# Seven-product pairs whose products add up in PSUM, and a sixth pair in the last projection

## The chip, the cores and the metric

The kernel runs on one core of one Trainium2 chip. The metric is the time of one execution on the device, in microseconds (us). TensorE (PE) does the matrix products into PSUM banks, VectorE (DVE) and ScalarE (ACT) read PSUM and do the elementwise work, GpSimd (POOL) and SyncE (SP) mainly issue transfers.

## The reference

Two layers over 640 tokens (512 latent, 128 context) with a model width of 2048. Each layer is a norm with a modulation, one wide input projection, two attention or convolution mixers with gates, an output projection, and a gated residual. What matters here is the output projection of each layer and its gated residual:

```python
    return jnp.concatenate([y_a, y_b], axis=-1) @ w_out, new      # even layer; the odd one alike
...
        xp = xp + gt_p * out_p
        xs = xs + gt_s * out_s
```

So both layers multiply a 640 x 2048 matrix y by a 2048 x 2048 matrix and add the product, times a gate for each column and token group, to x. The gate is one third of `modulation(...)`, a projection of the condition.

## The kernel before, in words

Everything is held transposed: features on the 128 partitions, the 640 tokens (`NT`) along the free dimension, in two halves of 320 (`HALF`). Accuracy near fp32 is had by splitting each operand into a high and a low part (`split`, L230 on ScalarE for the high part, L231 on VectorE for the low part) and using three matmuls: high x high, high x low, low x high. An output tile is 128 columns of the weights. A single tile (`proj_q`, L265 to L267) takes 16 slices of the contraction x 2 halves x 3 matmuls of 320 columns.

`project_out` (one call for each layer) runs the output projection. The first three tiles are led together while y comes in (`run_tiles`); then single tiles up to `N_SINGLE`, which is 4 in layer 0 and 6 in layer 1; then the other tiles in pairs (`run_pairs`): six pairs in layer 0, five in layer 1. A pair is two columns of tiles times two halves of tokens times two halves of the contraction, a 2 x 2 x 2 block product, done with seven products instead of eight by a Strassen-Winograd scheme. The seven are named Q1, Q2, N5, P6, P7, P4, Q3, and each is 8 slices x 3 matmuls (L515 to L517) into a bank of its own, in the order of the dictionary `MOV`. The weights enter as A11, A12, A21, A22 and as sums of them (`operand`, L451 to L461); the moving side are the halves of y (B11, B21, B22), the difference T1 and three sums T2, T3, T4.

`forms` makes T2 to T4 in eight steps: two loads of y from the scratch in HBM, four operations on VectorE (L1055 to L1058) and a split into the buffers T0 to T7. It runs as a generator in the queue `attn`, advanced between groups of matmuls of the leading tiles. In layer 1 it is put into the queue one group later (`y1_maker` at k = 4) than in layer 0 (`y0_maker` at k = 8 of the order 0, 2, 1, 3). T1 is split over one half of y (`t1`) when the last single tile has passed that half; for this the last single runs one half of the tokens and then the other. The room for `t1` and for what is kept between products are slices of `tables` (`room`).

What is done with a product stands in `after`: Q1 is copied to SBUF (L481), the others are combined on VectorE (L484 to L503) and added to the residual tile `xr` with the gate `hgt` (`res_sum`, L1072). Weight loads (`load8`, L427, in four buffers `w8`; `load_raw`, L243) are on SP, up to a pair ahead; splits are 3 half products ahead (`SPLIT_AHEAD`). When a pair of tiles is whole, layer 0 stores it and sums its squares (`x1_done`, `x1_last`), and layer 1 transposes and stores it (`rows_out`, `rows_last`). At the end of layer 0 the norm of the next layer follows half by half (`norm_half`), x1 is loaded back (`x1_tail`, `h1_maker`) and the next input projection begins.

The names are those of Tile's pools: instructions are put in order for each engine, and buffers handed out, when the program is built, so an engine's order follows the program with small shifts.

Of the kernel before, what the change touches and what calls it, by code (L numbers as in the profile page):

```python
# [20 lines left out]
P = 128  # L21
# [32 lines left out]
def trunk_kernel(ctx: ExitStack, tc: tile.TileContext, I: dict, O: dict):  # L54
# [81 lines left out]
    hgt = [const.tile([P, KT, 2], F32, name=f"hgt{l}") for l in range(2)]  # L136


    def ada_done(l, cb, h=0, n=4):
# [7 lines left out]
        elif which == 2:  # L147
            V.tensor_scalar(hgt[l][:, ks, :], mod[l][:, fs, :], 0.5, None, ALU.mult)

# [270 lines left out]
    def run_pairs(cols, w_ap, mov, room, begin, part, done, tail):  # L420
# [58 lines left out]
        def after(p, name, ps):  # L479
            if name == "Q1":  # L480
                A.copy(q1, ps)  # L481
                begin(p)
            elif name == "Q2":
                V.tensor_add(z, ps, q1)  # L484
                done(p, 0, 0, z)
            elif name == "N5":
                st8["n5"] = ps
            elif name == "P6":
                V.tensor_sub(u2, ps, q1)
                V.tensor_sub(u4, st8["n5"], u2)  # L490
                if p == len(cols) - 1:
                    part(p, 0, 1, u4)
            elif name == "P7":
                V.tensor_sub(z, ps, u4)
                done(p, 1, 1, z)
                V.tensor_add(u2, ps, u2)
                part(p, 1, 0, u2)
            elif name == "P4":
                done(p, 1, 0, ps)
            elif p == len(cols) - 1:  # L500
                done(p, 0, 1, ps)
            else:
                V.tensor_add(u4, ps, u4)  # L503
                done(p, 0, 1, u4)
# [4 lines left out]
        for i, (p, name) in enumerate(seq):  # L509
            ps, rows_ = pproj.tile([P, 512], F32, tag=f"p{'ab'[i % 2]}{i // 2 % 2}", name="pq")[:, 0:HALF], mov[MOV[name]]  # L510
            for h in range(2):
                wh, wl = parts[2 * i + h]
                for j in range(4):
                    hi, lo = rows_(4 * h + j)
                    PE.matmul(ps, wh[:, j, :], hi, start=(h == 0 and j == 0), stop=False)  # L515
                    PE.matmul(ps, wh[:, j, :], lo, start=False, stop=False)  # L516
                    PE.matmul(ps, wl[:, j, :], hi, start=False, stop=(h == 1 and j == 3))  # L517
# [971 lines left out]
```

## Time and profile before

| | us |
|---|---|
| median of three runs | 2333.07 (2333.01 to 2333.62) |
| the profiled execution | 2331.45 |
| its span in the profile | 2329.7 |
| TensorE busy | 2287.0 |
| VectorE busy | 1595.3 |
| ScalarE busy | 934.5 |
| GpSimd busy | 134.6 |
| pairs of layer 0, first matmul to last | 976.7 to 1126.1 |
| pairs of layer 1, first matmul to last | 2195.2 to 2324.8 |

The span runs from the first to the last instruction; the execution's own time has what lies around it too. Rows of the timeline begin with the start and the duration in us. A bracket at the end of a row tells how long the engine stood before it, and on what. In a view of groups, a row has the count, the busy time, the mean in ns, and the idle time ahead with the releaser. In a view of waits, a row has the sum, the count and the longest. The duration of a matmul's row reaches from its start to its modelled end, and rows of neighbouring matmuls overlap.

### The profile page before, as it was taken

Reading aid. Unit: us, or ns where it says so; the run is one execution under the profiler, and the core shown is the slowest. Engines: PE = TensorE matmul, PEld = TensorE weight load, DVE = VectorE, ACT = ScalarE, POOL = GpSimd, SP = SyncE. Lnnn points to the kernel's source line nnn. Section 1 sums busy time; section 2 is a strip of 40 time slices with the busy share of each in tenths; the row PEclk is TensorE's granted clock in tenths of the full one; section 3 lists DMA queues with packets and bytes.
Section 4 is the critical chain, followed back from the end, with each engine's and each line's share of the span. In section 5 each row is a group of like instructions: output and inputs, shape, how many; then the busy total and the mean of one; then the engine's idle time right before and its main releaser. Section 6 shows DMA issues by size and latency. Waiting matters only on the chain.

```text
span 2329.7 us, 41919 instructions
## 1 busy us (share of the span) xinstructions
PE 2287.0 (98%) x16116; PEld 2213.1 (95%) x16116; DVE 1595.3 (68%) x3270; ACT 934.5 (40%) x1963; POOL 134.6 (6%) x183
## 2 busy tenths in 40 slices
PE   7999999999999999999999999999999999999999
PEld 5889999999999999999999899999999999999999
DVE  4668887777777774988855755755856754568576
ACT  5334542433422222544554344444334444444343
POOL 1001000000000000000010100101000001000101
PEclk9999999999999999999999999999999999999999
DMA  9986345435455553844431422413423312128542
GB/s 322 293 263 200 102 116 176 146 105 171 128 169 166 170 165 124 274 135 137 152 98 55 132 82 70 145 52 98 120 72 97 103 46 82 46 74 274 179 121 70
DMA packets 399257, 321.99 MB, mean 138 GB/s; under 512 B 18882, under 2 KB 353184, under 8 KB 398544
## 3 DMA queue, kind: packets, MB, share of 16 engines
q1 hardware_dynamic: 391056, 288.94, 41.5%
q0 software_dynamic: 7280, 28.20, 3.3%
q8 instruction: 127, 2.08, 0.4%
q10 hardware_dynamic: 720, 2.16, 0.3%
q14 instruction: 74, 0.61, 0.1%
HBM read 290.79 MB, written 28.44 MB: 137 GB/s over the span
## 4 chain that ended last, share of the span: by engine, by line
PE 87%; DVE 5%; DMA 4%; ACT 2%; issue 1%; POOL 1%; SPq 0%; POOLq 0%; DVEq 0%; ACTq 0%
PE pa L265 10%; PE pb L266 10%; PE pb L265 10%; PE pb L267 10%; PE pa L266 10%; PE pa L267 10%; PE pq L515 4%; PE pq L517 4%; PE pq L516 4%; PE T L693 2%; PE S L705 2%; PE S L707 1%; PE S L706 1%; DMA yin<-yd 1%; PE T L167 1%
## 5 line engine op out<-in xcount | busy, mean ns | idle before, releaser
L230 ACT ACTIVATE wh<-raw 128x512 fp32r<-128x512 f32 (+1 forms) x510 | 307.4, 604 | 795.3 <-PE pb L266 673.5
L265 PE MATMUL pa<-h,wh 128*128 128x320 f32 x1760 | 561.9, 319 | 3.2 <-ACT h L230 1.6
L266 PE MATMUL pa<-h,wh 128*128 128x320 f32 x1760 | 547.2, 311 | 1.7 <-DVE h L231 1.6
L267 PE MATMUL pa<-h,wl 128*128 128x320 f32 x1760 | 545.8, 310 | 0.0
L267 PE MATMUL pb<-h,wl 128*128 128x320 f32 x1760 | 545.2, 310 | 0.0
L266 PE MATMUL pb<-h,wh 128*128 128x320 f32 x1760 | 544.9, 310 | 0.0
L265 PE MATMUL pb<-h,wh 128*128 128x320 f32 x1760 | 544.7, 310 | 0.0
L231 DVE TENSOR_TENSOR wl<-raw,wh 128x512 fp32r<-128x512 f32 (+1 forms) x510 | 333.3, 654 | 304.6 <-ACT wh L230 282.0
L202 DVE SCALAR_TENSOR_TENSOR acc<-adaw,sT,acc 128x512 f32<-128x512 f32 (+1 forms) x600 | 356.5, 637 | 23.3 <-DMA adaw<-in_ada_w 22.0
L265 PEld LDWEIGHTS pa<-h,wh 128*128 128x128 f32 x1760 | 331.9, 189 | 23.8 <-issue 17.0
L266 PEld LDWEIGHTS pa<-h,wh 128*128 128x128 f32 x1760 | 332.3, 189 | 4.9 <-DVE h L231 2.7
L267 PEld LDWEIGHTS pa<-h,wl 128*128 128x128 f32 x1760 | 331.9, 189 | 1.2 <-issue 1.2
L267 PEld LDWEIGHTS pb<-h,wl 128*128 128x128 f32 x1760 | 330.7, 188 | 0.8 <-issue 0.8
L266 PEld LDWEIGHTS pb<-h,wh 128*128 128x128 f32 x1760 | 330.6, 188 | 0.9 <-issue 0.8
L265 PEld LDWEIGHTS pb<-h,wh 128*128 128x128 f32 x1760 | 330.5, 188 | 0.7 <-issue 0.4
L679 ACT ACTIVATE p<-S,nm,rq 128x768 f32<-128x768 f32 (+3 forms) x120 | 101.2, 843 | 107.5 <-DVE nm L674 81.2
L515 PE MATMUL pq<-h,wh 128*128 128x320 f32 x352 | 109.9, 312 | 1.2 <-ACT wh L230 1.2
L516 PE MATMUL pq<-h,wh 128*128 128x320 f32 x352 | 108.8, 309 | 0.0
L517 PE MATMUL pq<-h,wl 128*128 128x320 f32 x352 | 108.5, 309 | 0.0
L672 DVE TENSOR_REDUCE nm<-S 128x1 f32<-128x768 f32 (+3 forms) x120 | 91.9, 765 | 21.7 <-PE S L707 20.2
L230 ACT ACTIVATE pth<-T 128x512 fp32r<-128x512 f32 (+1 forms) x132 | 66.0, 533 | 71.8 <-PE T L693 69.4
L231 DVE TENSOR_TENSOR ptl<-T,pth 128x512 fp32r<-128x512 f32 (+1 forms) x132 | 77.7, 608 | 6.7 <-ACT pth L230 5.4
(306 smaller groups left out, 3418.5 us busy)
## 6 DMA issues: line engine op xcount, KB each, us to landing
raw<-in_od_w_in SPq DMA_DIRECT2D x208, 256.0 KB, 2.9
adaw<-in_ada_w SPq DMA_DIRECT2D x192, 256.0 KB, 3.0
raw<-in_ev_w_in SPq DMA_DIRECT2D x176, 256.0 KB, 3.0
ada<-in_ada_w SPq DMA_DIRECT2D x32, 1024.0 KB, 7.7
adaw<-in_ada_w SPq DMA_DIRECT2D x128, 128.0 KB, 2.4
yd<-y POOLq DMA_DIRECT2D x34, 320.0 KB, 3.0
yin<-yd SPq DMA_DIRECT2D x32, 320.0 KB, 4.2
w<-yd SPq DMA_DIRECT2D x32, 320.0 KB, 4.1
```

The source lines that it names most:

```text
L202: V.scalar_tensor_tensor(out=a, in0=w, scalar=sT[:, kt, c:c + 1], in1=a, op0=ALU.mult, op1=ALU.add)
L230: A.activation(hi, x, AF.Copy)
L231: V.tensor_sub(lo, x, hi)
L265: PE.matmul(ps, wh[:, i, :], hi[:, sl], start=(j == js[0] if alone else (pos == 0 and j == 0)), stop=False)
L266: PE.matmul(ps, wh[:, i, :], lo[:, sl], start=False, stop=False)
L267: PE.matmul(ps, wl[:, i, :], hi[:, sl], start=False, stop=(j == js[1] - 1 if alone else (pos == 3 and j == 3)))
L515: PE.matmul(ps, wh[:, j, :], hi, start=(h == 0 and j == 0), stop=False)
L516: PE.matmul(ps, wh[:, j, :], lo, start=False, stop=False)
L517: PE.matmul(ps, wl[:, j, :], hi, start=False, stop=(h == 1 and j == 3))
L672: V.tensor_reduce(nm, s, axis=AX.X, op=ALU.max, negate=True)
L679: A.activation(p[:, 0:n], s, AF.Exp, scale=rsc, bias=nm, accum_out=l)
L693: PE.transpose(t[:, i * P:(i + 1) * P], p, ident)
```

## The change

The seven products get another order: Q1, N5, P6, Q2, P7, Q3, P4. Q1, P6, P7 and P4 add up in one bank (`pa0` or `pa1`, in turn from pair to pair), N5 and Q3 in `pb0`, Q2 in `pb1`. Only Q1, N5 and Q2 start a bank anew. Between the products of a chain ScalarE copies the partial sum to SBUF (after Q1, N5, P6 and P7), and VectorE adds copies where two chains meet (after Q2, P7 and Q3). For this the signs change: the forms T2 to T4 are made with other signs (two of the four operations are now `scalar_tensor_tensor`), the second tile of a pair comes out negated and takes a negated gate `nhgt`, and the two halves of the tokens swap roles (`HX`). The last product of a pair is P4 in place of Q3. The last single tile runs its halves in the other order. In layer 1 `N_SINGLE` becomes 4: two single tiles become a sixth pair. At the end of layer 0 the row of norm factors lies in `sf` in place of `T3`, and the reloads of x1 change buffers accordingly.

```diff
+            V.tensor_scalar(nhgt[l][:, ks, :], mod[l][:, fs, :], -0.5, None, ALU.mult)
...
-        MOV = {"Q1": "B11", "Q2": "B21", "N5": "T1", "P6": "T2", "P7": "T3", "P4": "T4", "Q3": "B22"}
+        MOV = {"Q1": "B11", "N5": "T1", "P6": "T2", "Q2": "B21", "P7": "T3", "Q3": "B22", "P4": "T4"}
+        BANK = {"N5": "pb0", "Q3": "pb0", "Q2": "pb1"}
...
-        q1, z, u2, u4 = room
+        q1, n5, u2, u3 = room
...
+            elif name == "N5":
+                A.copy(n5, ps)
+            elif name == "P6":
+                A.copy(u2, ps)
             elif name == "Q2":
-                V.tensor_add(z, ps, q1)
-                done(p, 0, 0, z)
-            elif name == "N5":
-                st8["n5"] = ps
-            elif name == "P6":
-                V.tensor_sub(u2, ps, q1)
-                V.tensor_sub(u4, st8["n5"], u2)
-                if p == len(cols) - 1:
-                    part(p, 0, 1, u4)
+                V.tensor_add(q1, ps, q1)
+                done(p, 0, 0, q1)
             elif name == "P7":
-                V.tensor_sub(z, ps, u4)
-                done(p, 1, 1, z)
+                A.copy(u3, ps)
+                V.tensor_add(n5, u3, n5)
+                done(p, 1, 1, n5)
+            elif name == "Q3":
                 V.tensor_add(u2, ps, u2)
-                part(p, 1, 0, u2)
-            elif name == "P4":
+                done(p, 0, 1, u2)
+            else:
                 done(p, 1, 0, ps)
-            elif p == len(cols) - 1:
-                done(p, 0, 1, ps)
-            else:
-                V.tensor_add(u4, ps, u4)
-                done(p, 0, 1, u4)
...
-            ps, rows_ = pproj.tile([P, 512], F32, tag=f"p{'ab'[i % 2]}{i // 2 % 2}", name="pq")[:, 0:HALF], mov[MOV[name]]
+            bank, rows_, new = BANK.get(name, f"pa{(p + 1) % 2}"), mov[MOV[name]], name in ("Q1", "N5", "Q2")
+            if new:
+                banks[bank] = pproj.tile([P, 512], F32, tag=bank, name="pq")[:, 0:HALF]
+            ps, kw = banks[bank], {} if new else {"skip_group_check": True}
...
-            elif name == "P4":
+            elif name == "Q3":
                 load(p + 1, "A21")
                 load(p + 1, "A22")
-            if name in ("P6", "P7") and p == len(cols) - 1:
+            if name in ("Q2", "P7") and p == len(cols) - 1:
                 tail(name)
...
-    N_SINGLE = (4, 6)
+    N_SINGLE = (4, 4)
...
+    HX = (1, 0)
...
-            b11, b12, b21, b22 = ya[:, 0:HALF], ya[:, HALF:NT], yb[:, 0:HALF], yb[:, HALF:NT]
+            b11, b12, b21, b22 = (t[:, HV[h][1]] for t in (ya, yb) for h in HX)
...
-            V.tensor_sub(x3, b12, b22)
-            V.tensor_sub(x2, b11, x3)
-            V.tensor_sub(x4, b21, x2)
+            V.tensor_sub(x3, b22, b12)
+            V.scalar_tensor_tensor(out=x2, in0=x3, scalar=-1.0, in1=b11, op0=ALU.mult, op1=ALU.subtract)
+            V.scalar_tensor_tensor(out=x4, in0=x2, scalar=-1.0, in1=b21, op0=ALU.mult, op1=ALU.subtract)
             V.tensor_sub(d, b11, b12)
...
-            for hv in ([HV] if n < n0 - 1 else [HV[1:], HV[:1]]):
+            for hv in ([HV] if n < n0 - 1 else [[HV[HX[1]]], [HV[HX[0]]]]):
...
-            part(p, t, h, src)
+            n, h = n0 + 2 * p + t, HX[c]
+            res_sum(l, n, src, CS[1:] if h else CS[:1], nhgt if t else hgt)
...
-            st["rbc"] = big("T3")[:, 0:NT]
+            st["rbc"] = big("sf")[:, 0:NT]
...
-                for i in range(3 if g < 2 else 2):
-                    x1_back(6 + 3 * g + i, t, i)
+                for i in range(3):
+                    x1_back(5 + 3 * g + i, t, i)
```

More of the change, by code (lines that the diff above doesn't have):

```diff
@@ L136, in trunk_kernel @@
     hgt = [const.tile([P, KT, 2], F32, name=f"hgt{l}") for l in range(2)]
+    nhgt = [const.tile([P, KT, 2], F32, name=f"nhgt{l}") for l in range(2)]
     def ada_done(l, cb, h=0, n=4):
@@ L416, in run_tiles, with run_pairs @@
             begin(fn, pp)
-    def run_pairs(cols, w_ap, mov, room, begin, part, done, tail):
+    def run_pairs(cols, w_ap, mov, room, begin, done, tail):
         ap = pools["cur"]
@@ L1157, in project_out @@
                   {"B11": half_of(0, 0), "T1": half_of(0, 1), "B21": half_of(8, 0), "B22": half_of(8, 1),
-                   "T2": form_of(0), "T3": form_of(1), "T4": form_of(2)}, room, begin, part, done, tail)
+                   "T2": form_of(0), "T3": form_of(1), "T4": form_of(2)}, room, begin, done, tail)
         drain(prep)
@@ L1223, in x1_tail @@
     def x1_tail(name):
[L1225 to L1226 removed]
+        for k in (range(0, 4) if name == "Q2" else (4,)):
+            x1_back(k, big("w8", bufs=4) if k < 4 else big("sx"))
     def x1_back(k, t, i=0):
@@ L1422, in rows_last @@
         n = KT - 2 + t
-        if t:
+        if not t:
             if h == 0:
```

27 lines of the change are left out of this document (11 added, 16 removed).

## The prediction

> **What bounds the kernel now.** I read the page first, for the engine that fills the span and for the chain that ended last.
>
> ```profile
> span 2329.7 us, 41919 instructions
> PE 2287.0 (98%) x16116; PEld 2213.1 (95%) x16116; DVE 1595.3 (68%) x3270; ACT 934.5 (40%) x1963; POOL 134.6 (6%) x183
> PE 87%; DVE 5%; DMA 4%; ACT 2%; issue 1%; POOL 1%; SPq 0%; POOLq 0%; DVEq 0%; ACTq 0%
> ```
>
> TensorE is busy for 2287.0 of 2329.7 us and carries 87% of the chain. No other engine is near that. So time comes out only with matmuls, or out of the 42.7 us in which TensorE stands. The next view, busy time by stretch, shows the two pair stages alone, layer 0 and then layer 1.
>
> ```profile
> core 0: us, PE busy (x) PEld busy (x) DVE busy (x) ACT busy (x) POOL busy (x), PEclk, DMA share, GB/s
> 976.66:1126.10 149.44, 149.44 (x1022) 149.35 (x1022) 124.30 (x208) 63.52 (x105) 7.35 (x13) 1.00 0.51 150
> 2195.16:2324.80 129.64, 129.38 (x894) 128.62 (x892) 91.92 (x155) 51.14 (x93) 12.65 (x20) 1.00 0.33 98
> ```
>
> Inside the stages TensorE is busy for 149.44 of 149.44 and 129.38 of 129.64 us, at granted clock 1.00. VectorE has 124.30 and 91.92 us of work, ScalarE 63.52 and 51.14. So fewer VectorE operations inside a pair gain nothing, and copies put on ScalarE lie beside matmuls. What TensorE waits for near the projections is in the waits, first from 900 to 1180 us (layer 0), then from 2100 us on (layer 1).
>
> ```profile
> PE T L1216 <- POOL r L1212: 1.4, 1, 1.4
> PE pq L515 <- ACT wh L230: 1.2, 1, 1.2
> ```
>
> ```profile
> PE pa L266 <- DVE h L231: 1.0, 1, 1.0
> PE T L1431 <- DVE xr L1072: 0.6, 1, 0.6
> PE T L544 <- ACT ot L1411: 0.6, 2, 0.3
> PE T L1431 <- issue: 0.2, 1, 0.2
> ```
>
> Layer 0 has one stall of 1.2 us where its pairs begin (L515). Layer 1 has none there. The others lie ahead of the pairs or in the tail.
>
> **The count of matmuls.** In layer 1, tiles 4 and 5 were single: 2 x 16 x 2 x 3 = 192 matmuls. As a pair they take 7 x 24 = 168. The price of one is the distance between starts, not the 0.31 us in a row, since matmuls overlap.
>
> ```profile
> 2200.58 0.31 PE L517 MATMUL pq<-h,wl 128*128 128x320 f32 x1
> 2202.78 0.31 PE L517 MATMUL pq<-h,wl 128*128 128x320 f32 x1
> ```
>
> These two are 15 matmuls apart: 2.20 / 15 = 0.1467 us. So a product of 24 takes 3.52 us, and the change removes exactly one: **-3.52 us**. A chain that continues in a bank adds nothing to that: 23 of a product's 24 matmuls accumulate already at this pitch. Layer 0 keeps its six pairs, and the output transposes keep their number. By the Trainium skill, page "TensorE: Matmul & The Clock Gate", section "Back-to-back issue gap", a warm matmul alone takes N/2.4 + 2.5 = 136 ns for 320 columns; by that estimate the 24 would be worth 3.26 us and the time 0.26 us more. The trace's 0.1467 us decides.
>
> **The work between products.** Durations, from the groups of the layer 1 stage and from the lines' own rows:
>
> ```profile
> L489 DVE TENSOR_TENSOR tables<-pq,tables 128x320 f32<-128x320 f32 x5 | 2.5, 491 | 2.1 <-PE pq L517 2.1
> L1072 DVE SCALAR_TENSOR_TENSOR xr<-tables,hgt,xr 128x320 f32<-128x320 f32 x10 | 5.5, 545 | 0.0
> L231 DVE TENSOR_TENSOR wl<-w,wh 128x512 fp32r<-128x512 f32 x17 | 11.7, 687 | 1.6 <-ACT wh L230 1.5
> L230 ACT ACTIVATE wh<-w 128x512 fp32r<-128x512 f32 x17 | 10.8, 632 | 18.5 <-PE pq L516 17.4 <-PE pa L266 1.1
> L481 ACT COPY tables<-pq x11: 407/410/427, 980.8 to 2302.9; 128x320 f32<-128x320 f32 x11
> L1055 DVE TENSOR_TENSOR sx<-w,w x16: 478/484/491, 929.6 to 2159.0; 128x320 f32<-128x320 f32 x16
> ```
>
> Per pair VectorE loses three adds of 0.49 us (six to three) and one residual sum (seven to six), some 2 us; ScalarE gains three copies of 0.41 us (1.2 us). With ScalarE at 51 of 130 us both cost nothing while the matmuls cover them. New are TensorE's waits on a bank that a copy still reads: P6 behind the copy of Q1, P7 behind P6's, P4 behind P7's, Q3 behind N5's. At least one whole product (N5, Q2, Q3) of 3.52 us lies between each. A copy queued behind one split ends 0.63 + 0.41 = 1.04 us after its product, so I take these waits at nothing, with 2.5 us of cover. Behind P7's copy VectorE waits with its add, and residual sums, operand adds and low splits queue behind that; they waited there for P7 itself before. Loads: the weights A21 and A22 of the next pair are now needed for the second product instead of the third, but Q3's add of A12, which frees a buffer for A21, comes one product earlier too, so the load has about four products, as before. The negated gate (nhgt) adds tiny operations beside other work: nothing.
>
> **The start of the pairs, layer 0.** Here is the stall that exists, so I followed it through all engines' timelines.
>
> ```profile
> 968.28 1.01 SPq L427 DMA_DIRECT2D w<-in_ev_w_out  x2
> 971.11 0.63 SPq L427 DMA_DIRECT2D w<-in_ev_w_out  x1
> 970.79 1.16 DVE L231 TENSOR_TENSOR T<-sx,T 128x960 fp32r<-128x960 f32 x1
> 973.28 1.15 ACT L230 ACTIVATE wh<-w 128x512 fp32r<-128x512 f32 x2 [2.17 <-DMA w<-in_ev_w_out]
> 974.27 0.48 DVE L231 TENSOR_TENSOR h<-w,h 128x320 fp32r<-128x320 f32 x1
> 975.20 0.31 PE L267 MATMUL pa<-h,wl 128*128 128x320 f32 x1
> 975.26 0.68 DVE L231 TENSOR_TENSOR wl<-w,wh 128x512 fp32r<-128x512 f32 x1
> 975.98 1.15 ACT L230 ACTIVATE wh<-w 128x512 fp32r<-128x512 f32 x2 [1.54 <-DMA w<-in_ev_w_out]
> 976.66 0.41 PE L515 MATMUL pq<-h,wh 128*128 128x320 f32 x1 [1.15 <-ACT wh L230]
> w<-in_ev_w_out SPq DMA_DIRECT2D x4, 512.0 KB, 6.2
> ```
>
> The last single ends at 975.2. The first pair matmul runs at 976.66, just behind the third high split: that of A12, the second product, since the first product's bank pa0 was still to be read by the last single's sum. After the change Q1 goes to pa1, free for long, and needs A11 only, whose high splits end at 974.43 and first low split at 975.94. That removes up to 1.2 us. Against it, two of four operations in each of the eight form steps become 0.545 instead of 0.484 us: 16 x 0.061 = 0.98 us more on VectorE, which is full until the pairs begin. The forms, the eight last splits (end 974.75) and Q1's low split then come about 1 us later, at 976.9. I take 1.0 us of stall instead of 1.2: **-0.2**. N5 comes second now: A21, issued by 971.74, lands 6.2 us later at 977.9; an add (0.68, as a split of that size) and a high split (0.63) make 979.2, and N5 is due at 976.2 + 3.52 = 979.7. It just fits, with 0.5 us to spare. If A21 instead gets the buffer that the last split frees (974.75 + 0.98 = 975.7), it is ready at 975.7 + 6.2 + 1.3 = 983.2, 3.5 us late. That is the upper bound.
>
> **The start of the pairs, layer 1.** Today two more singles (29 us) lie between the forms and the pairs; this cover goes.
>
> ```profile
> 2149.64 0.39 PE L265 MATMUL pa<-h,wh 128*128 128x320 f32 x1
> 2156.20 0.38 SPq L427 DMA_DIRECT2D w<-in_od_w_out  x1
> 2159.16 2.05 SPq L427 DMA_DIRECT2D w<-in_od_w_out  x2
> 2161.58 1.16 DVE L231 TENSOR_TENSOR T<-sx,T 128x960 fp32r<-128x960 f32 x1
> 2165.76 0.31 PE L267 MATMUL pb<-h,wl 128*128 128x320 f32 x1
> w<-in_od_w_out SPq DMA_DIRECT2D x3, 512.0 KB, 6.6
> ```
>
> Tile 3 runs from 2149.6 to 2165.9 and becomes the last single. The forms end at 2162.7. They get 0.98 us slower, and about two low splits of tile 4 (1.4 us) leave VectorE: 2162.3. In layer 0 the remaining splits ended 2.8 us after the last form (974.75 against 971.95), so 2165.1, and Q1's low split 2165.8: I take a stall of 0.4 us, **+0.4**. A21 is out by 2161.2, lands 6.6 us later at 2167.8, is added and split by 2169.1; N5 is due at 2166.3 + 3.52 = 2169.8. In the wrong buffer: 2165.1 + 6.6 + 1.3 = 2173.0, so 3.2 us late, the upper bound here. The lower bound is no stall. On SP the raw loads of tiles 4 and 5 (2 MB) go, which can only bring these loads forward.
>
> **The ends.** The last product is P4 in place of Q3, again with two sums read from its bank and the same transposes behind it: nothing. In layer 0 half of the norm now starts behind Q3 with its add (0.49 us) in front, under P4's 3.52 us: nothing, and 0.5 us if that cover is gone. The reloads of x1 number 0 to 3 stay behind the fourth product; those into T buffers go out a product (3.52 us) later on SP, since P4 reads all T to its end.
>
> ```profile
> 1140.01 0.74 DVE L1251 SCALAR_TENSOR_TENSOR T<-sf,gsc,T 128x512 f32<-128x512 f32 x1
> ```
>
> The first of them, x1 number 5, is used at 1140.0, 13.9 us after the last product (1126.1), so they stay hidden; the raw loads behind them on SP go out equally later and have the same slack.
>
> **Sum:** -3.52 - 0.2 + 0.4 = -3.3 us. The profiled execution took 2331.45 us by the clock of the runs (span 2329.7), so it would take 2328.1. It lies 1.6 us below the median of 2333.07; moved to the median, the forecast is **2329.8 us**. A difference of 0.2% (4.67 us) is about what a measurement of this kernel can tell from no change, and the forecast is inside it.
>
> **The rivals.**
>
> Clean starts. Both starts run without a stall: -3.52 - 1.2 = -4.7 us, 2328.3, just past 0.2%. For it: the bank conflict goes. Against it: VectorE is full before the pairs.
>
> Late N5. A21 takes the buffer of the last form input in both layers: +3.5 and +3.2 us on top of -3.3 at most, so 2329.8 to 2336.5. For it: the slack is only 0.5 and 0.7 us. Against it: in both layers the trace shows that load going out before the last split frees its buffer.
>
> Re-entry waits, the slower case. ScalarE executes in its written order; if a copy is written behind splits that themselves wait for TensorE to free a weight buffer, the chain's next product stands.
>
> ```profile
> ACT wh L230 <- PE pq L516: 51.2, 50, 1.2
> 2225.23 0.63 ACT L230 ACTIVATE wh<-sx 128x512 fp32r<-128x512 f32 x1 [1.02 <-issue]
> 2225.77 0.41 ACT L481 COPY tables<-pq 128x320 f32<-128x320 f32 x1
> ```
>
> Such waits last up to 1.2 us, 50 times. A copy behind three splits, two of which wait, ends 3 x 0.63 + 2 x 1.2 + 0.41 = 4.7 us after its product, 1.2 beyond the cover. There are four re-entries in each of 12 pairs: 48 x 1.2 = 58 us, 2388. It decides from 0.17 us per re-entry on ((4.67 + 3.3) / 48). Against it: in the rows above the copy of Q1 runs behind one split. By the Trainium skill, page "PSUM — Partial Sum Buffer", section "PSUM bank collisions raise a hardware error", a bank must be guarded between engines as a whole, so none of these waits can be dodged; no run here shows a collision.
>
> That the change does not do what it says would need a pair to cost as much as two singles; the pitch in the rows above leaves no room for that, and I give it nothing.
>
> **Chances and range.** Forecast 0.52, clean starts 0.18, late N5 0.18, re-entry waits 0.12. Faster by over 0.2%: clean starts and the low edge of the forecast, 0.20. Slower by over 0.2%: 0.12; late N5 stays below +4.67 us. Within 0.2%: 0.68. The range 2328.0 to 2334.0 leaves out the re-entry waits (0.12), the last part of late N5 (0.04) and 0.03 below.
>
> **What would show it.** Right: TensorE has 24 matmuls fewer and the layer 1 pair stage is one pair longer; TensorE busy in both pair stages as fully as now; the waits of the chained products on ScalarE's copies absent; stalls of about 1.0 and 0.4 us at the two starts. Wrong: a wait of a pair's matmul on a copy or on VectorE that recurs twelve times, a gap ahead of N5 of the first pair with a weight load behind it, or a slower form stage that holds up tile 3 itself.

## The result, and the profile after

The changed kernel takes 2335.54 us (median of 16 runs) beside 2331.51 us for the kernel before (16 runs on the same chip): a ratio of 1.0017, 95% interval 1.0010 to 1.0025. That is 4.0 us slower, where 3.3 us less had been forecast: the forecast of 2329.8 us and its range of 2328.0 to 2334.0 start from the first three runs of the kernel before (median 2333.07). The profiled execution took 2336.23 us, with a span of 2334.4 us, 4.7 us over the span before.

From the page of the changed kernel:

```profile
span 2334.4 us, 41910 instructions
PE 2286.5 (98%) x16092; PEld 2209.1 (95%) x16092; DVE 1591.4 (68%) x3246; ACT 950.3 (41%) x2006; POOL 134.4 (6%) x183
```

TensorE has the 24 matmuls less (16092 for 16116), yet only 0.5 us less busy time, and a longer span: it stands longer, and some of what it does goes slower. (Lines from the pair code on have moved by one to three: the pair matmuls are now L516 to L518, the output transposes L545, the residual sum L1074, the copy of transposes out of PSUM L1409, the large weight loads L429, N5's two adds L453, the forms L1057 to L1060.)

TensorE's waits of the changed kernel, from 900 to 1180 us (layer 0, two of its rows):

```profile
PE pq L518 <- DVE wl L233: 0.8, 2, 0.7
PE pq L516 <- ACT wh L232: 0.4, 1, 0.4
```

and from 2100 us on (layer 1):

```profile
PE T L545 <- DVE xr L1074: 3.4, 1, 3.4
PE T L545 <- ACT ot L1409: 2.1, 1, 2.1
PE pa L268 <- DVE h L233: 1.8, 2, 1.4
PE T L1429 <- DVE xr L1074: 0.6, 1, 0.6
```

The stall of 1.2 us at L515 in layer 0 is gone, and short waits at the second and third product have come. Layer 1 has two single waits that were not there: 3.4 us of the output transposes for a residual sum, and 2.1 us for the copy of transposes out of PSUM. Both lie between 2150 and 2175 us. The timeline of the changed kernel around them:

```profile
2153.02 1.00 ACT L232 ACTIVATE T<-sx 128x960 fp32r<-128x960 f32 x1 [3.24 <-DVE sx L1059]
2153.93 0.57 ACT L1409 COPY ot<-T 128x512 f32<-128x512 f32 x1
2154.55 0.77 PE L545 MATMUL T<-ident,xr 128*128 128x128 f32 x5 [2.10 <-ACT ot L1409]
...
2157.01 1.19 SPq L429 DMA_DIRECT2D w<-in_od_w_out  x2
2158.29 3.76 SPq L1069 DMA_DIRECT2D xr<-xd  x1
2162.45 0.49 DVE L1059 SCALAR_TENSOR_TENSOR sx<-sx,w 128x320 f32<-128x320 f32 x1
2162.96 10.88 SPq L429 DMA_DIRECT2D w<-in_od_w_out  x3
2164.01 1.16 DVE L233 TENSOR_TENSOR T<-sx,T 128x960 fp32r<-128x960 f32 x1 [0.67 <-ACT T L232]
...
2171.01 1.29 DVE L453 TENSOR_TENSOR sx<-w,raw 128x512 f32<-128x512 f32 x2 [3.87 <-issue]
2173.36 0.67 DVE L1074 SCALAR_TENSOR_TENSOR xr<-pb,hgt,xr 128x192 f32<-128x192 f32 x2
2173.83 0.90 PE L545 MATMUL T<-ident,xr 128*128 128x128 f32 x3 [3.36 <-DVE xr L1074]
```

This is one chain. ScalarE holds the copy of finished transposes behind a form's split, which waits 3.24 us for VectorE: TensorE stands 2.10 us. The last form's operation at 2162.45 ends at 2162.94 and so frees the buffer of A21, whose load goes out at 2162.96 and lands 8.0 us later, at 2170.9. VectorE stands 3.87 us ahead of N5's adds, which need A21 and begin at 2171.01, and the residual sum of tile 3 is written behind these adds: it runs at 2173.36, and the transposes of tile 3, written into Q1, wait 3.36 us for it. Q1 itself had begun on time (2168.32).

After that wait TensorE is slow for a while, as the busy time by stretch shows (columns as in the prediction's table; the seventh group is the granted clock):

```profile
2170.40:2173.30 2.90, 0.06 (x1) 0.00 (x0) 2.29 (x3) 1.25 (x2) 0.00 (x0) 1.00 0.04 11
2173.30:2176.80 3.50, 2.97 (x12) 2.98 (x13) 3.15 (x6) 0.97 (x3) 1.29 (x2) 0.51 0.59 164
```

Over 3.5 us the granted clock is 0.51, and TensorE starts 12 instructions where it starts 24 otherwise. The matmuls there stand 0.27 us apart in place of 0.147, nine of them: 1.1 us more.

Last, a small wait in every pair of layer 1, from the answer on line L545 of the changed kernel, 2201 to 2330 us:

```profile
its engine sat idle before it (us, times) until:
  PE pq L518: 1.2, 4
```

The kernel before has no such row. A pair takes 25.96 us between the same instructions of two pairs (2201.41 and 2227.37) in place of 25.72 (2221.07 and 2246.79 in the kernel before).

**How stretches are compared below.** Single executions of one kernel differ by some 11 us (2324.2 to 2335.2 us for the kernel before in one session), so a ratio is known to about 0.1%, 2.3 us, and that is the size of what is sought. So the traces are also compared by stretch: the start of TensorE's matmul number 14,400 (in layer 1's lead, at 2073.8 us before), of the 900th from the end (just ahead of the last five pairs, 2194.4) and of the last one. "Start" is the length of the first stretch against the kernel before, with 3.52 us added for kernels with six pairs, which have 24 matmuls less in it; "pairs" is that of the second. The changed kernel: 125.08 - 120.62 + 3.52 = 8.0 us for "start", 0.6 for "pairs".

| kernel | median, us | ratio to before, 95% | start, us | pairs, us |
|---|---|---|---|---|
| changed | 2335.54 | 1.0017 (1.0010-1.0025) | 8.0 | 0.6 |
| e1_five_pairs | 2332.05 | 1.0011 (1.0002-1.0020) | 0.6 | 0.6 |
| e2_six_pairs_old | 2334.45 | 1.0019 (1.0010-1.0028) | 8.2 | -0.2 |
| e3_a21_first | 2335.98 | 1.0029 (1.0017-1.0040) | 7.9 | 0.6 |
| e4_n5_third | 2333.86 | 1.0015 (1.0005-1.0025) | 7.9 | 0.6 |
| e5_one_load | 2332.32 | 1.0010 (1.0000-1.0021) | 3.3 | 0.6 |
| e6_less_dve | 2332.01 | 1.0008 (0.9997-1.0018) | 2.9 | 0.6 |
| e7_a12_in_raw | 2332.70 | 1.0016 (1.0004-1.0028) | 6.1 | 0.4 |
| e8_later_twice | 2334.10 | 1.0012 (1.0002-1.0022) | 4.3 | -0.6 |
| e9_after_again | 2334.96 | 1.0023 (1.0013-1.0033) | 6.0 | 0.6 |
| e10_form_on_pool | 2339.52 | 1.0042 (1.0027-1.0058) | 10.2 | 0.6 |
| e11_three_edits | 2335.89 | 1.0025 (1.0014-1.0035) | 7.0 | -0.6 |
| e12_raw_too | 2332.86 | 1.0013 (1.0002-1.0024) | 4.6 | -0.6 |
| e13_spread | 2336.50 | 1.0027 (1.0016-1.0038) | 7.2 | 0.6 |
| e14_combined | 2330.96 | 1.0001 (0.9993-1.0010) | 3.5 | -0.6 |
| e15_combined_five | 2330.34 | 0.9995 (0.9987-1.0004) | -1.6 | -0.4 |
| e16_before_again | 2330.35 | 0.9998 (0.9989-1.0008) | 0.3 | 0.0 |

The medians of before in the four later sessions were 2330.08, 2330.34, 2330.32 and 2331.15 us. "Pairs" repeats to 0.1 us; "start" repeats to about 2 us (8.0 and 6.0 for the changed kernel itself).

Part of "start" is the granted clock. Within that stretch the traces of e3, e11 and e13 have 6.8 us at a clock of 0.50, e10 two times 3.4 us, the changed kernel, e2, e4, e8, e9 and e12 3.4 us, and the kernel before, e1, e5, e6, e7, e14, e15 and e16 none. In the changed kernel's trace this was worth 1.1 us, so differences of 1 us between rows of the table, and of 2 us where 6.8 us are slow, can be the clock alone.

### The profile page after: what moved, and what is told of

It is laid out like the page before. It is cut to its first block, busy times and chain, and to the rows that moved or that the text cites. A ratio compares the mean times of both kernels' runs of the same rounds, so it can differ in the third digit from the quotient of the medians.

```text
span 2334.4 us, 41910 instructions
## 1 busy us (share of the span) xinstructions
PE 2286.5 (98%) x16092; PEld 2209.1 (95%) x16092; DVE 1591.4 (68%) x3246; ACT 950.3 (41%) x2006; POOL 134.4 (6%) x183
## 4 chain that ended last, share of the span: by engine, by line
PE 48%; DVE 4%; DMA 3%; ACT 1%; issue 1%; POOL 0%; SPq 0%; DVEq 0%; POOLq 0%; ACTq 0%
PE pa L267 4%; PE pb L268 4%; PE pb L267 4%; PE pb L269 4%; PE pa L269 4%; PE pa L268 4%; PE pq L518 4%; PE pq L517 4%; PE pq L516 4%; PE T L694 1%; DMA adaw<-in_ada_w 1%; PE S L706 1%; PE S L708 1%; PE S L707 1%; DMA yin<-yd 1%
## 5 line engine op out<-in xcount | busy, mean ns | idle before, releaser
L267 PE MATMUL pa<-h,wh 128*128 128x320 f32 x1728 | 551.5, 319 | 3.5 <-ACT h L232 3.0
L268 PE MATMUL pa<-h,wh 128*128 128x320 f32 x1728 | 537.4, 311 | 2.8 <-DVE h L233 2.8
L269 PE MATMUL pa<-h,wl 128*128 128x320 f32 x1728 | 535.5, 310 | 0.0
L269 PE MATMUL pb<-h,wl 128*128 128x320 f32 x1728 | 535.0, 310 | 0.0
L268 PE MATMUL pb<-h,wh 128*128 128x320 f32 x1728 | 534.9, 310 | 0.0
L267 PE MATMUL pb<-h,wh 128*128 128x320 f32 x1728 | 534.6, 310 | 0.0
L267 PEld LDWEIGHTS pa<-h,wh 128*128 128x128 f32 x1728 | 325.4, 188 | 24.6 <-issue 16.6
L268 PEld LDWEIGHTS pa<-h,wh 128*128 128x128 f32 x1728 | 326.1, 189 | 6.3 <-DVE h L233 4.2
L269 PEld LDWEIGHTS pa<-h,wl 128*128 128x128 f32 x1728 | 325.6, 188 | 1.2 <-issue 1.2
L268 PEld LDWEIGHTS pb<-h,wh 128*128 128x128 f32 x1728 | 324.4, 188 | 0.9 <-issue 0.8
L267 PEld LDWEIGHTS pb<-h,wh 128*128 128x128 f32 x1728 | 324.3, 188 | 0.8 <-issue 0.4
L516 PE MATMUL pq<-h,wh 128*128 128x320 f32 x384 | 119.7, 312 | 0.4 <-ACT wh L232 0.4
L518 PE MATMUL pq<-h,wl 128*128 128x320 f32 x384 | 119.2, 310 | 0.7 <-DVE wl L233 0.7
L517 PE MATMUL pq<-h,wh 128*128 128x320 f32 x384 | 119.2, 310 | 0.0
L516 PE MATMUL pq<-T,wh 128*128 128x320 f32 x288 | 89.5, 311 | 0.1
```

The source lines that it names most:

```text
L267: PE.matmul(ps, wh[:, i, :], hi[:, sl], start=(j == js[0] if alone else (pos == 0 and j == 0)), stop=False)
L268: PE.matmul(ps, wh[:, i, :], lo[:, sl], start=False, stop=False)
L269: PE.matmul(ps, wl[:, i, :], hi[:, sl], start=False, stop=(j == js[1] - 1 if alone else (pos == 3 and j == 3)))
L516: PE.matmul(ps, wh[:, j, :], hi, start=(new and h == 0 and j == 0), stop=False, **kw)
L517: PE.matmul(ps, wh[:, j, :], lo, start=False, stop=False, **kw)
```

## The experiments

### Chains or sixth pair: e1_five_pairs, e2_six_pairs_old

e1 is the changed kernel, e2 the kernel before, each with only this line edited:

```diff
e1:  -    N_SINGLE = (4, 4)
     +    N_SINGLE = (4, 6)
e2:  -    N_SINGLE = (4, 6)
     +    N_SINGLE = (4, 4)
```

> The changed kernel with the last projection back at two more single tiles and five pairs (192 matmuls in place of 168, 3.52 us more); chains, order and form signs stay changed. Theory 'cover': what went wrong in layer 1 is that the two singles no longer lie over the forms and the load of A21, so N5's adds, the residual sum of tile 3 and the transposes stand (2.1 + 3.4 us, and 1.1 us at a lower clock behind them). Then this kernel loses only the gap of about 0.2 us in each of five pairs and the later start of N5 in layer 0 (1.4 us, partly made up later): 1.0 to 2.5 us above the kernel before, about 2 us below the changed kernel; no TensorE wait over 1 us at the start of layer 1's pairs. Rival 'chains': the order and the copies of the pairs cost it in all of them; then this kernel is 3.5 us or more above the changed one, about 7.5 us above the kernel before.

> The kernel before with only the sixth pair in the last projection: old order (N5 third), sums on VectorE, no chains. Theory 'cover, with N5 second': A21 has one product (3.5 us) more, so little of the 3.4 us stall and of the lower clock behind it is there: -3.5 + 0.8 (later forms) + 0 to 2 us, that is 2.7 to 0.7 us below the kernel before. Theory 'cover alone': any six-pair kernel pays for the missing singles: 1 to 4 us above the kernel before. Rival 'chains': the sixth pair is a pure gain in the old order, 3.5 us below.

The longest waits of layer 1, of e1 and then of e2:

```profile
PE pa L268 <- DVE h L233: 1.1, 1, 1.1
```

```profile
PE pq L517 <- DVE wl L231: 3.3, 1, 3.3
PE T L544 <- ACT ot L1411: 2.1, 1, 2.1
PE pa L266 <- DVE h L231: 1.6, 1, 1.6
```

With the two singles back, both waits go and the start costs 0.6 us. With the old order and no chains, but six pairs, it costs 8.2 us, as in the changed kernel: the same 2.1 us, and 3.3 us for a weight split in place of the residual sum. So the chains do not make it, and neither does N5's place in the order, which I had blamed; the sixth pair does, in any order. What the new order and its chains cost is 0.6 us in the pairs (and about 1.5 us in layer 0, below); "chains cost 3.5 us and more" is out. The medians fit, though their intervals overlap: e2 is 1.0019 of the kernel before, and e1 is still 1.0011, 2.6 us, for which the traces have 1.5 in layer 0, 0.6 at the start and 0.6 in the pairs. So of the 4.0 us of the changed kernel a good part stays when the sixth pair is taken out again; what the sixth pair does is to lose more than the 3.52 us that it saves.

### The order of the first loads and products: e3_a21_first, e4_n5_third

```diff
e3:  -        for n in ("A11", "A12", "A21", "A22"):
     +        for n in ("A11", "A21", "A22", "A12"):
e4:  +        FIRST = ("Q1", "Q2", "N5", "P6", "Q3", "P7", "P4")
     -        seq = [(p, n) for p in range(len(cols)) for n in MOV]
     +        seq = [(p, n) for p in range(len(cols)) for n in (MOV if p else FIRST)]
```

> The changed kernel with the first pair's loads issued as A11, A21, A22, A12 in place of A11, A12, A21, A22, in both layers. Theory 'cover': A21 lands 2 to 4 us earlier, N5's adds no longer hold VectorE, the 3.4 us wait of the transposes behind tile 3's residual sum and the 1.1 us at lower clock go for the most part, and so does most of 2.3 us of waits at the start of layer 0's pairs: 3 to 6 us below the changed kernel, 2 us below to 1 us above the kernel before. The 2.1 us wait of tile 3's transposes on the copy out of PSUM stays. Rival 'chains': within 0.5 us of the changed kernel.

> The changed kernel with the first pair of each layer in the order Q1, Q2, N5, P6, Q3, P7, P4 (N5 third, as before); the other pairs stay. P7 and P4 then follow each other in one bank with no product between: a wait for P7's copy of 0.4 us (nothing queued) to 1.1 us (one split ahead of it) in each layer, which prices a re-entry without cover. Theory 'cover': A21 has 3.5 us more, so the waits ahead of N5 and the 3.4 us wait of the transposes go for the most part; less the re-entry, 2 to 5 us below the changed kernel. Rival 'chains': the two re-entries only, 0.8 to 2.2 us above the changed kernel.

Both missed: the start costs 7.9 us in either. In e3 the adds come sooner and VectorE stands 4.45 us for A21 in front of the last form's split instead; in e4 it stands 3.06 us ahead of N5's adds, and the transposes wait 3.4 us again. In these two traces an order that only moves the wait along one chain gained nothing. (In e3 6.8 us of the start ran at half the clock, in the changed kernel 3.4, so a gain of about 1 us may hide there; its median, 1.0029, shows none.)

e4 also priced a re-entry of a bank with no product between. Its timeline, where P7 ends (997.68) and P4 follows in the same bank (998.94):

```profile
997.68 0.31 PE L519 MATMUL pq<-T,wl 128*128 128x320 f32 x1
997.83 0.30 PE L517 MATMUL pq<-h,wh 128*128 128x320 f32 x1
...
998.70 0.31 PE L517 MATMUL pq<-h,wh 128*128 128x320 f32 x1
998.94 0.42 PE L517 MATMUL pq<-T,wh 128*128 128x320 f32 x1
998.48 0.41 ACT L496 COPY tables<-pq 128x320 f32<-128x320 f32 x1
```

From P7's last matmul to P4's first 1.26 us pass, 1.1 us more than the pitch: that is one uncovered re-entry, with a split ahead of the copy, which began 0.8 us after P7's last matmul. The program's order on TensorE had put seven matmuls of the next pair's Q1 in between, so only 0.2 us was lost.

### Loads or VectorE: e5_one_load, e6_less_dve

```diff
e5:  -        for n in ("A11", "A12", "A21", "A22"):
     -            load(0, n)
     +        load(0, "A11")
     +        st8[0, "A12"] = st8[0, "A21"] = st8[0, "A11"]
     +        st8[0, "A22"] = halves(st8[0, "A11"])
e6:  -            split(t[:, 0, :], t[:, 1, :], x)
     +            if "fin" in pools:
     +                A.activation(t[:, 0, :], x, AF.Copy)
     +                A.activation(t[:, 1, :], x, AF.Copy)
     +            else:
     +                split(t[:, 0, :], t[:, 1, :], x)
```

The condition on `"fin"` in e6 holds in layer 1 alone.

> The changed kernel where the first pair of each layer loads only A11 and uses that tile also as A12, A21 and A22: 1.5 MB of loads left out per layer, so the output of that pair is another; every VectorE, ScalarE and TensorE operation stays. All six-pair kernels so far lost about 8 us between the lead's last tile and the second pair of layer 1, whatever their order. Theory 'loads': the last 4.5 us of it (the wait for A21 and its adds, and the lower clock behind it) come from the first pair's loads, which go out only when the forms free their buffers; here VectorE's idle 3.9 us before N5's adds and the 3.4 us TensorE wait go, 4 to 5 us of the 8. Theory 'VectorE': its work (forms, splits, adds), squeezed into one single tile in place of three, sets the time; then the loss stays above 6.5 us.

> The changed kernel where, in layer 1 only, the low half of each form's split is a copy on ScalarE in place of a subtraction on VectorE (8 x 1.16 = 9.3 us less on VectorE before the pairs, about 8 us more on ScalarE; the low halves hold the whole value, so the output differs). Theory 'VectorE': the 8 us lost at the start of layer 1's pairs shrink by 5 us or more. Theory 'loads': the 2.1 us wait behind the copy out of PSUM shrinks, since ScalarE waits for VectorE there, and the loads go out as much earlier as the forms end earlier; the rest stays: 2 to 4 us less.

The waits of layer 1, three rows of e5 and then two of e6:

```profile
PE T L546 <- ACT ot L1410: 1.3, 1, 1.3
PE T L546 <- DVE xr L1075: 1.0, 1, 1.0
PE pq L519 <- DVE wl L233: 0.8, 1, 0.8
```

```profile
PE T L545 <- ACT ot L1413: 2.1, 1, 2.1
PE pa L268 <- DVE h L233: 0.8, 2, 0.4
```

Each takes a large part of it away: 3.3 us are left with the loads left out, 2.9 with VectorE relieved, beside 8.0 and 6.0 in the two profiles of the changed kernel. About 1.1 us of the gain is the slow stretch, which neither has. The medians point the same way (1.0010 and 1.0008 for 1.0017), within their intervals. So the two are not rivals but links of one chain: the forms end on VectorE, that frees buffers, the loads go out, they land 6.5 to 8 us later, N5's adds follow. Shortening either link shortens the chain. Against the first profile e6 went further than the loads theory allowed (5.1 us, not 2 to 4), against the second it did not (3.1); with the forms early, the residual sum no longer waits for A21.

### Links one by one: e7_a12_in_raw, e8_later_twice, e9_after_again

```diff
e7:  -            if name == "A22":
     -                st8[p, name] = [load_raw(w_ap, c1, qd) for qd in (2, 3)]
     +            if name in ("A12", "A22"):
     +                st8[p, name] = [load_raw(w_ap, c1 if name == "A22" else c0, qd) for qd in (2, 3)]
     ...
     -        for n in ("A11", "A12", "A21", "A22"):
     +        for n in ("A11", "A21", "A22", "A12"):
e8:           def later(n):
     +            yield
                  yield
                  finish(n)
```

> The changed kernel with A12 loaded in two parts into the small weight buffers that A22 uses, and the first loads in the order A11, A21, A22, A12: all values as in the changed kernel. A21 then takes the second buffer that the forms free and not the third (issue at about 2157 in place of 2163 us), A12 buffers that tile 3 leaves. Theory 'loads, by buffers': N5's operand comes 3 to 5 us earlier, the 8 us shrink to 4 to 5, and layer 0 loses its 1.4 us: 4 to 6 us below the changed kernel, 0 to 2 us below the kernel before. Theory 'loads, by bandwidth' (the DMA share is 0.9 to 1.05 from 2100 to 2170 us): the same bytes come no earlier, within 1 us of the changed kernel. Theory 'VectorE': within 1 us too.

> The changed kernel with the output transposes of a finished tile started one half product later, in all pairs. The gap of 0.2 us before them in each pair of layer 1 (TensorE reaches the transposes before the residual sum that follows Q3's add) then goes: 0.6 to 1.2 us less between the second pair of layer 1 and the end. If the gap has another cause, such as the matmuls' own pitch in a continued chain, it stays at 0.2 us per pair.

> The changed kernel once more, with a second profile. From the lead's last matmuls of layer 1 to the second pair, the kernels with six pairs and all loads have lost 8.0, 8.2, 7.9, 7.9, 6.1 and 4.3 us against the kernel before. If that loss belongs to the kernel, it is 7 to 9 us here again; if it hangs on how long the loads of A11 to A22 happen to take (6.5 to 8 us), anything from 4 to 9 us.

e7 got 6.1 us: 2 us less than the first profile of the changed kernel, but no less than its second (6.0, e9). Its A21 did go out early, at 2156.57, but took 9.6 us, and the program's order put the sum that reads it ahead of the last form's split, as in e3:

```profile
2166.21 1.23 DVE L458 TENSOR_TENSOR sf<-w,w 128x1024 f32<-128x1024 f32 x1 [4.12 <-DMA w<-in_od_w_out]
```

So the wait moved here too. e8's edit touches the start only by the 0.2 us at the end of the first pair, yet its start is 4.3 us, and e9's 6.0. Part of that is how long the load of A21 happens to take, 8.0 us in the changed kernel's first profile, 7.5 in e9 and 6.5 in e8: the transposes' wait for the residual sum is 3.4, 2.9 and 1.3 us. But of the 2.0 us between the two profiles of the changed kernel that makes 0.5; 1.3 is a wait of the lead for a split of y (L268, 1.8 and 0.5 us). In the pairs e8 did what was expected: 0.6 us less than before in place of 0.6 us more, 1.15 us, and the row "until PE pq L518" is gone. The gap was the residual sum of a pair's first tile, which now needs Q3's add before it.

### A form's operation on GpSimd: e10_form_on_pool, e11_three_edits, e12_raw_too

```diff
e10: -            V.tensor_sub(d, b11, b12)
     +            G.tensor_tensor(d, b11, b12, op=ALU.subtract)
```

e11 is e10 with e8's edit and, in layer 0, e3's order; e12 is e11 with A12 loaded as in e7 (in layer 1 the order stays A11, A12, A21, A22).

> The changed kernel with one of the four operations of each form (the difference b11 - b12) on GpSimd in place of VectorE, in both layers; same values. VectorE has 8 x 0.49 = 3.9 us less before each layer's pairs. Chain theory (the forms end on VectorE, that frees the buffers, that starts the loads, then N5's adds, then tile 3's transposes): the loss at the start of layer 1's pairs shrinks by 2 to 4 us, to 4 to 6. Rival 'loads by bandwidth': no change from the changed kernel (6 to 8 us). If GpSimd's operation takes over 2 us, or holds VectorE up, the forms end later and the loss grows.

> The changed kernel with the form's difference on GpSimd, the output transposes of a pair half a product later, and in layer 0 the first loads in the order A11, A21, A22, A12; same values. Chain theory: layer 0 loses its 1 to 2 us, layer 1's start loses 2 to 4 of its 8 us and the pairs 1.1 us: 4 to 7 us below the changed kernel, 0 to 3 us below the kernel before. Rival 'loads by bandwidth': 2 to 3 us below the changed kernel, 1 to 2 us above the kernel before.

> The kernel e11_three_edits with A12 loaded in two parts into the small weight buffers as well, so that A21 takes the second buffer that the forms free; same values. Chain theory: another 1 to 3 us less at the start of layer 1's pairs than there, 1 to 5 us below the kernel before. Rival 'loads by bandwidth': within 1 us of e11_three_edits.

The timeline of e10 at one of the forms (GpSimd's difference and VectorE's operations of the same length of 320), with the same operation of the next form, and the longest wait of layer 1:

```profile
2153.38 0.88 POOL L1060 TENSOR_TENSOR sf<-w 128x320 f32<-128x320 f32 x1 [4.48 <-DMA w<-yd]
2153.47 1.13 DVE L1057 TENSOR_TENSOR sx<-w,w 128x320 f32<-128x320 f32 x1
...
2159.01 0.48 DVE L1057 TENSOR_TENSOR sx<-w,w 128x320 f32<-128x320 f32 x1
...
2166.17 0.54 POOL L1412 DMA_DIRECT2D out_y_prompt<-ot  x1
2166.72 0.90 POOL L1060 TENSOR_TENSOR w<-w 128x320 f32<-128x320 f32 x1
```

```profile
PE T L545 <- ACT ot L1409: 4.0, 1, 4.0
```

The operation takes 0.9 to 1.5 us on GpSimd, under the 2 us that I had named as harmful. But the VectorE operation that starts beside it takes 1.13 us in place of 0.48: the 0.49 us that left VectorE comes back as 0.65. At other forms another operation is struck, by about as much (a weight split at 2128.31 takes 1.37 us in place of 0.69). And the last difference, queued on GpSimd behind two output transfers, comes at 2166.72, after VectorE's last form operation (2166.34). The wait for the copy grew from 2.1 to 4.0 us and the start to 10.2: relief on paper, load in fact. e11 missed what either theory gave it: 1.0025, a start of 7.0 us and a wait for the copy of 3.8. e12 gained on e11 what was expected (2.4 us at the start), but stayed above the kernel before (1.0013): no wait for A21 is left in it, but that for the copy remains with 3.4 us.

### All that helped, with and without the sixth pair: e13_spread, e14_combined, e15_combined_five, e16_before_again

```diff
e13:  in the last single's half passes
     -                    go_on()
     +                    if len(hv) == 2 or qd % 2:
     +                        go_on()
```

e14 is the changed kernel with this, e8's edit, A12 as in e7, and in layer 0 the order A11, A21, A22, A12; e15 is e14 with `N_SINGLE = (4, 6)`; e16 is the kernel before.

> The changed kernel with the output work of the lead's three tiles taken up every second quarter of tile 3's half passes in place of every one, so that 24 matmuls and not 12 lie between two sets of transposes; all values as there. If the density makes the 2.1 us wait (transposes for the copy that ScalarE holds behind a form's split), that wait falls below 0.5 us and the loss at the start of layer 1's pairs (8.0 and 6.0 us in two profiles) falls by 1 to 2 us. If VectorE's fullness makes it, it comes back at another place: the loss stays at 6 to 8 us.

> The changed kernel with four edits, values as there: A12 loaded in two parts into the small weight buffers; in layer 0 the first loads in the order A11, A21, A22, A12; the output transposes of a pair half a product later; the spread of e13_spread. Chain theory: the loss at the start of layer 1's pairs falls to 1 to 3 us, layer 0 loses nothing, the pairs 0.55 us less than before: -3.5 + 1 to 3 - 0.55, 3 to 1 us below the kernel before. Rival 'any six-pair kernel pays': loss of 4 us or more, 0 us or above.

> The kernel e14_combined with two more single tiles and five pairs in the last projection. Both theories: no loss at the start of layer 1's pairs, 0.5 us less in them: 1 us below to 0.5 us above the kernel before. Chain theory: it is 0.5 to 2.5 us above e14_combined; the rival: at or below it.

> The kernel before once more, for a second profile. Its stages (layer 0's lead and pairs, layer 1's lead, the start of layer 1's pairs) should repeat within about 1 us each; where one differs by more, differences of that size between two traces say nothing there.

The waits of layer 1, the longest of e13 and then three of e14:

```profile
PE T L545 <- DVE xr L1074: 4.7, 1, 4.7
```

```profile
PE pa L268 <- DVE h L233: 1.8, 2, 1.6
PE T L546 <- DVE xr L1075: 1.0, 1, 1.0
PE pq L519 <- DVE wl L233: 0.6, 1, 0.6
```

In e13 the 2.1 us wait is gone and the other has grown from 3.4 to 4.7: density gave it its place, not its size, and the start still costs 7.2 us, about 2 of them at the lower clock. In e14, with A21 earlier as well, 3.5 us are left. That is 3.52 us saved and 3.5 lost (the pairs gain 0.6, the first pair of layer 0 with 26.1 us loses about 1): e14 stands at 1.0001 (0.9993 to 1.0010) of the kernel before, and the same kernel with five pairs at 0.9995 (0.9987 to 1.0004). The 0.5 to 2.5 us by which five pairs were to be slower did not show. So the four edits give back what the change lost, but e14 did not reach the 1 to 3 us below it that were expected, and no version here beats the kernel before by more than can be measured. e16 shows how a trace of the same kernel repeats: 0.3 us in the start, but 1.5 us in layer 0 and the norm behind it.

## Why the prediction was wrong, point by point

**-3.52 us for the matmuls: right.** 24 fewer, at the same pitch; a continued chain costs nothing by itself (the last five pairs of layer 0 take 124.3 us, 124.4 before).

**Re-entry waits: right that there are none.** No row of a pair's matmul waiting for a copy exists in any stretch. That rival (2388 us) needed copies behind three splits; with no product between, a re-entry cost 1.1 us (e4), and there is one product or more in every case.

**The work between products at nothing: off by +0.6 us.** The prediction named the row that would show a recurring wait, but looked for it at the matmuls. It sits at the transposes, for which the residual sum behind Q3's add is late by 0.2 us in each pair.

**Forms 0.98 us slower in each layer: wrong, and it did not matter.** The two changed operations took 0.49 us, as before; the 0.545 us row was of an operation with another third operand. The forms ended later all the same (2165.17, the end of the last split, in place of 2162.74): the lead ended 0.8 us later, and seven of the eight low splits of T1, which used to stand 20 us behind the forms (2182.84 on), were put between the last of them.

**Layer 0, -0.2 us: wrong.** The stall ahead of Q1 is gone, as the bank argument had it, and not reduced to 1.0 us. But N5, due 3.52 us after Q1's start, began at 980.19 in place of 979.34, and P6 and their weights came in small waits. A21, issued at 971.18, landed 7.5 us later and was added from 978.72 on. The sum had taken 6.2 us, the median of four loads, though the load in A21's place took 7.4 in the trace before:

```profile
w<-in_ev_w_out SPq DMA_DIRECT2D x1, 512.0 KB, 7.4
```

The first pair, from its first matmul to that of the second, takes 27.3 us, in the kernel before 24.7. Six kernels with the changed kernel's layer 0 average +1.3 us (-0.2 to 2.2) against the first profile of before from the 6,400th matmul (902 us) to the 9,200th (1323 us), three profiles with the old one -0.2 us (-1.5 to 0.9). So the term is about +1.5 us, known to 1 us. The first pair alone, 26.1 to 27.3 us in those six and 24.7 to 25.4 in the three, holds all of it.

**Layer 1, +0.4 us: the step that failed.** It measured 6 to 8 us. In the first trace that is 2.1 for the copy, 3.4 for the residual sum, 1.1 at the lower clock and 0.8 more in the lead (L268, 1.8 for 1.0), with 0.6 not placed; the stall that the 0.4 stood for, ahead of Q1, did not come. The cover that the two singles gave (29 us) was named, but only N5 was checked against it, with slacks of 0.5 and 0.7 us from times of the trace before. Three things were left out. Tile 3 became the last single, run in half passes, so the forms' last steps, the splits of T1, its own weights and the transposes of three tiles fell into 18 us in place of 46. VectorE is busy for 9.96 of the 10 us from 2150 to 2160, 9.37 in the kernel before. A21's load then went out 1.8 us later than "by 2161.2", and took 8.0 us, not 6.6 (the median of three loads). A21's own load, in the changed kernel and in the kernel before:

```profile
w<-in_od_w_out SPq DMA_DIRECT2D x1, 512.0 KB, 8.0
w<-in_od_w_out SPq DMA_DIRECT2D x1, 512.0 KB, 6.9
```

Why it was slower is open: the DMA share from 2160 to 2170 is 1.05, in the kernel before 1.07. And the wait did not strike N5 but what stands behind N5's adds on VectorE: the residual sum, and so the transposes, half a product earlier, with a lower clock after. The bound of 3.2 us for a late A21 was thus no bound.

**Late N5, given 0.18,** was the nearest case, but its condition did not come true. A21 took the buffer that the last form's operations free, as in the kernel before (2160.53, behind the operation that ends at 2160.50); the one behind the last split (2165.56) went to another load at 2165.60. A21 was late in its usual buffer. The rival's time, up to 2336.5, holds the measured 2335.54, but by a sum with other terms: layer 0 gave about 1.5 us of its 3.5, layer 1 twice its 3.2. That the measured time falls into it is luck. The argument against it, that A21's load goes out before the last split, held; it was no reason to take a late A21 for excluded, since the trace was one in which two singles hid everything behind it.

By the measured terms: -3.5, + 1.5 in layer 0, + 6 to 8 at the start, + 0.6 in the pairs: 4.6 to 6.6, beside the 4.0 us (2.3 to 5.8) of the medians and 4.7 of the spans.

## What to carry to other kernels

When a change takes out work that nothing waits for, ask what ran underneath it: list everything that must now end in the shorter time on each engine and queue, not only the operand that the next step needs. A late operand is felt first by what is written behind its consumer on the same engine. And the same chain can be broken at any link (buffers, loads, VectorE): in the traces here a fix that reordered it only moved the wait, while a shorter link helped.

## What the hardware showed that was not expected

The granted clock falls to half after short pauses, but not after each of them. Two stretches of e8, a pause of 2.0 us and what follows, and then two of the kernel before, a pause of 3.0 us and what follows (columns as above):

```profile
2150.00:2152.70 2.70, 0.69 (x7) 0.69 (x7) 2.66 (x7) 2.22 (x5) 0.45 (x1) 1.00 0.78 255
2152.70:2156.10 3.40, 3.40 (x15) 3.36 (x14) 3.40 (x9) 3.40 (x10) 2.09 (x4) 0.50 0.87 297
```

```profile
1336.00:1339.00 3.00, 0.04 (x1) 0.00 (x0) 3.00 (x8) 0.61 (x2) 0.59 (x1) 1.00 0.07 22
1339.00:1342.40 3.40, 3.25 (x22) 2.99 (x23) 3.40 (x9) 1.35 (x4) 0.00 (x0) 1.00 0.66 196
```

15 matmuls and transposes in 3.4 us after the shorter pause, 22 after the longer. In all traces the slow stretches last 3.4 or 6.8 us (but for one at the very end of the kernel), and within a trace their starts lie whole multiples of 3.4133 us apart: 207.97, 1129.57 and 2327.64 us in the kernel before, 270 and 621 multiples behind the first. Divided into windows on this grid, e8's pause lies in one (2149.30 to 2152.71, TensorE busy for 41% of it), the longer one of the kernel before in two (from 1334.37 and 1337.78, 49% and 60%). In the 18 traces from 50 us on, each of the 46 windows at full clock with TensorE busy for under 45% was followed by a slow one, and 9 of the 26 with 45 to 54%. Of the 11878 busier ones 13 were, all between 1124 and 1130 us, at the end of layer 0, and why is open. So what counts is not the length of the pause but the idle time in one window. The Trainium skill, page "TensorE: Matmul & The Clock Gate", section "What's actually happening", says that activity is judged in free-running windows of 3413 ns; the lengths and the grid agree. The same page's section "HAM oscillation — how this bites in real kernels" asks for no pauses over about 3.4 us. Here 2.0 us was enough, so a pause of 2 us carries a risk of up to 1.7 us more (half of 3.4). Part of the spread between executions goes with this: in the four later sessions those of the kernel before with a mean granted clock of 0.999 took 2328.4 us on average (32 of them), with 0.998 2330.1 (66), with 0.997 2332.7 (25).

The other surprise stands at e10: a GpSimd operation on 128 x 320 floats lengthens the VectorE operation that starts beside it, 1.13 us for 0.48; one of 0.69 us takes 1.37 (2128.31), one of 0.82 takes 1.50 (2125.82), so about 0.7 us each time. The Trainium skill, page "GPSIMD Engine Reference", section "1. Specifications", says that GpSimd shares its SBUF interfaces with VectorE and contends with VectorE's instructions that have two SBUF inputs; e10 agrees, and gives the price.
